# Attention in pairs of heads as blocks of TensorE's order, and small tables loaded later on another queue, in a hybrid decoder layer

## The chip, the cores and the metric

One core of a Trainium2 chip runs the whole layer in one launch. The metric is the device time of that core in microseconds (us). The kernel before took 1037.85 us (median of three runs, 1037.11 to 1038.55).

The engines are named as the profile names them: PE (TensorE matmul) and PEld (its weight loads), DVE (VectorE), ACT (ScalarE), POOL (GpSimd), SP (SyncE, which issues most DMAs). A "weight matmul" below is a matmul of one of the big projections. "fp32r" is the single-pass format of the split operands; a plain fp32 matmul shows as two records (two passes) in the trace.

## What is computed

One layer over 256 tokens and 2048 channels. An RMS norm feeds one input projection (`w_in`) whose columns are the inputs of three branches and their gates: (A) attention with 8 heads of 128, (B) attention with 16 query heads of 64, 4 key/value heads, a window of 128 and sinks, (C) a short convolution with a gated linear recurrence. Each branch is multiplied by a SiLU gate and projected, the sum goes through `w_out`, and a second gated stage and a final norm follow. With 256 tokens both attentions are, for the later 128 queries, scores against all 256 keys, and for the first 128 queries scores against 128 keys. Cut to the attention of branch B:

```python
s = einsum('bnqhgd,bnlhd->bhgnql', qb, kband) * scale + bias
s = where(mask, s, NEG)
p = softmax(concatenate([s, sink_col], -1), -1)[..., :-1]
out = einsum('bhgnql,bnlhd->bnqhgd', p, vband)
```

The bias is a table of 32 buckets per head, looked up by distance.

## The kernel before

All projections are fp32 matmuls done as three fp32r matmuls (`mm3`, L114): each operand is split into a high part (a cast on ACT, L110 for weights) and a low part (a subtraction on DVE, L111), and hi·hi, hi·lo and lo·hi are summed in PSUM. `project_turned` (L157) does the same for results with channels in the rows, with one 512-column matmul (L164) and one 256-column matmul (L166). A weight tile of 1024 columns is loaded by SP into one of four `wraw` buffers, split into one of four `wsp` buffers, and feeds 12 weight matmuls of 512 columns. The code is written stage by stage; a scheduler that simulates the engines then fixes each engine's order, so that small matmuls of the attentions stand between weight matmuls of the merge that runs at the same time (`merge`, L574: branch C's merge around attention A, branch A's merge around attention B). An engine runs its list strictly in order.

`attention` (L431) takes heads two by two (`ha`), but each head of a pair has its own steps on PE: scores (L451, `mm3` of 256 columns, and L452, a plain fp32 matmul of 128 columns for the first 128 queries) into `s_`, softmax (L456 to L476 on DVE and ACT), three transposes of 128x128 (L479) into `pt_`, copies and a split of the result, then the values (L490 to L496) into `py_`. In branch B (`dh` = 64) the scores use 64 rows of the array, the upper half for one head and the lower half for the other; the values fill 64 columns; the second head of a pair skips the split and uses plain fp32 matmuls (L495, L496). All small PSUM tiles (`aux`, L68) share four buffers.

At the start seven dummy matmuls `busy` (L261) run while the first data come. POOL issues the loads of the small tables `tab`, `convw`, `sinkb` (L83, L301) there, and of `onehot` and `maskv` (L318, L319) in the second chunk of the input projection, where a list of hooks (L346) puts small work between weight tiles.

Of the kernel before, what the change touches and what calls it, by code (L numbers as in the profile page):

```python
# [11 lines left out]
F32 = mybir.dt.float32  # L12
# [34 lines left out]
def trunk(ctx: ExitStack, tc: tile.TileContext, x, xt, p, table, onehot, maskv, w_in, sinks, conv, w_ri, vec, fin, w_br,  # L47
# [31 lines left out]
    nc.vector.memset(half_c, -0.5)  # L79

    def load(src, n, name, parts=P):
        t = const.tile([parts, n], F32, name=name)
        nc.gpsimd.dma_start(t, src)  # L83
        return t
# [84 lines left out]
    def unit(name):  # L169
        return block(f"{name}_hi", F32R), block(f"{name}_lo", F32R)  # L170
# [129 lines left out]
    sinkb = const.tile([P, NB], F32, name="sinkb")  # L300
    nc.gpsimd.dma_start(sinkb, bass.AP(tensor=sinks.tensor, offset=sinks.offset, ap=[[0, P], [1, NB]]))  # L301
    acc = temp("acc").rearrange("p k t -> p (k t)")
# [39 lines left out]
    def decay():  # L342
        softplus_neg(sp8)
        nc.vector.tensor_scalar_mul(sp8, sp8, LRU_C)

    second_ps = in_chunk(hooks={2: lambda: squares(0), 4: lambda: squares(1), 6: lambda: squares(2), 8: lambda: squares(3),  # L346
                                10: norm_rows, 12: bias_rows, 14: decay})
# [82 lines left out]

    def attention(nheads, dh, qk_of, row_of, v_of, gate, bias0, sink, name):  # L431
        z = unit(f"z{name}")
        per = P // dh
        st = [small.tile([P, nheads, NH], F32, tag=f"st{i}{name}", name=f"st{i}{name}", bufs=1) for i in range(3)]
        den, mx, sk = st
        q_last = k_last = v_last = None
        for h0 in range(0, nheads, 4):
            bias = bias_tile(bias0 + h0, 4, f"bias_{name}{h0}")
            for ha in (h0, h0 + 2):
                pr = slice(ha, ha + 2)  # L440
                es = []
                for j in range(2):
                    (q, k), rows_of = qk_of(ha + j), row_of(ha + j)
                    if q is not q_last:
                        q_last = q
                        qs = split_small(q[:, P:SEQ], f"q_{name}{ha + j}", "q", P)
                    if k is not k_last:
                        k_last = k
                        ks = split_small(k, f"k_{name}{ha + j}")
                    sc = aux(f"s_{name}{ha + j}")  # L450
                    mm3(sc[:, :SEQ], [t[rows_of] for t in qs], [t[rows_of] for t in ks], True, True)  # L451
                    nc.tensor.matmul(sc[:, SEQ : SEQ + P], q[rows_of, 0:P], k[rows_of, 0:P], start=True, stop=True)  # L452
                    e = small.tile([P, SEQ + P], F32, tag="e", name=f"e_{name}{ha + j}", bufs=4)
                    b = bias[:, ha - h0 + j]
                    for c, (o, w, rev) in enumerate(((0, SEQ, b[:, ::-1]), (SEQ, P, b[:, P - 1 :: -1]))):
                        nc.vector.tensor_tensor_reduce(e[:, o : o + w], sc[:, o : o + w], rev, op0=ALU.add, op1=ALU.max,  # L456
                                                       scale=1.0, scalar=-3.0e38,
                                                       accum_out=mx[:, ha + j, c : c + 1])
                    es.append(e)
                if sink is not None:  # L460
                    nc.vector.tensor_tensor(mx[:, pr], mx[:, pr], sink[:, pr].unsqueeze(2).to_broadcast([P, 2, NH]), op=ALU.max)
                    nc.vector.tensor_tensor(sk[:, pr], sink[:, pr].unsqueeze(2).to_broadcast([P, 2, NH]), mx[:, pr], op=ALU.subtract)
                    nc.scalar.activation(sk[:, pr], sk[:, pr], AF.Exp)
                nc.vector.tensor_scalar_mul(mx[:, pr], mx[:, pr], -1.0)
                for j in range(2):
                    for c, o, w in ((0, 0, SEQ), (1, SEQ, P)):
                        nc.scalar.activation(es[j][:, o : o + w], es[j][:, o : o + w], AF.Exp,
                                             bias=mx[:, ha + j, c : c + 1], accum_out=den[:, ha + j, c : c + 1])
                if sink is not None:
                    nc.vector.tensor_add(den[:, pr], den[:, pr], sk[:, pr])  # L470
                nc.vector.reciprocal(den[:, pr], den[:, pr])
                py = aux(f"py_{name}{ha}")
                for j in range(2):
                    e = es[j]
                    for c, o, w in ((0, 0, SEQ), (1, SEQ, P)):
                        nc.vector.tensor_scalar_mul(e[:, o : o + w], e[:, o : o + w], den[:, ha + j, c : c + 1])  # L476
                    pt = aux(f"pt_{name}{ha + j}")
                    for c, o in enumerate((SEQ, 0, P)):
                        nc.tensor.transpose(pt[:, c * P : (c + 1) * P], e[:, o : o + P], ident)  # L479
                    v0, v1 = v_of(0, ha + j), v_of(1, ha + j)  # L480
                    part = slice(j % per * dh, (j % per + 1) * dh)
                    o = j // per * SEQ
                    if part.start == 0:
                        w1 = small.tile([P, P], F32, tag="w1", name=f"w1_{name}{ha + j}")
                        nc.scalar.copy(w1, pt[:, SEQ : SEQ + P])
                        w0 = split_small(pt[:, :SEQ], f"w0_{name}{ha + j}", "w")
                        if v0 is not v_last:
                            v_last = v0
                            vs = split_small(v0, f"v_{name}{ha + j}", "v", dh)
                        mm3(py[part, o : o + SEQ], vs, w0, True, False)  # L490
                    else:
                        w = small.tile([P, SEQ + P], F32, tag="w", name=f"w_{name}{ha + j}")
                        nc.scalar.copy(w, pt[:, : SEQ + P])
                        w1 = w[:, SEQ:]
                        nc.tensor.matmul(py[part, o : o + SEQ], v0, w[:, :SEQ], start=True, stop=False)  # L495
                    nc.tensor.matmul(py[part, o + P : o + SEQ], v1, w1, start=False, stop=True)  # L496
                n = 2 // per
                kt = ha // per
                nc.vector.tensor_tensor(gate[:, cols(kt, n)], py[:, : n * SEQ], gate[:, cols(kt, n)], op=ALU.mult)
                split_act(z, kt, n, gate[:, cols(kt, n)])  # L500
        return z
# [13 lines left out]
    def branch_a(between):  # L515
        qT, kT, g = block("qa"), block("ka"), block("ga")
        turned(ktiles(qT), 4, DA ** -0.5)
        between()
        turned(ktiles(kT), 4)
        between()  # L520
        silu(ktiles(g), 2, "ga0")
        between()
        silu(ktiles(g)[:, 4:, :], 2, "ga1")
        va = [[vh[:, c, h * DA : (h + 1) * DA] for h in range(NA)] for c in range(NH)]
        qa, ka = ([ktiles(t)[:, h, :] for h in range(NA)] for t in (qT, kT))
        return attention(NA, DA, lambda h: (qa[h], ka[h]), lambda h: slice(0, P),
                         lambda c, h: va[c][h], g, 0, None, "a")

    def branch_b():
# [7 lines left out]

        def kv_of(h):
            return B_ORDER[h] // (NB // NKV)

        def part(h):
            return slice(h % 2 * DB, (h % 2 + 1) * DB)

        qb = [ktiles(qT)[:, i, :] for i in range(NB // 2)]
        kb = [kT[:, i, :] for i in range(2)]
        vb = [[vt[:, c, i * DB : (i + 1) * DB] for i in range(NKV)] for c in range(NH)]

        return attention(NB, DB, lambda h: (qb[h // 2], kb[kv_of(h) // 2]), part,
                         lambda c, h: vb[c][kv_of(h)], g, NA, sinkb, "b")

# [208 lines left out]
```

## Time and profile before

| | |
|---|---|
| median of three runs | 1037.85 us |
| the profiled execution's own time | 1037.24 us |
| its span, first to last instruction | 1035.5 us |
| PE busy | 1022.5 us (99%) |
| DVE, ACT, POOL busy | 637.9, 537.6, 43.6 us |
| attention B on PE | 540 to 702 us, among weight matmuls |
| attention A on PE | 255 to 366 us |

The profiled execution is 0.61 us below the median. Matmuls are pipelined: a record's own length overlaps the next one, so a matmul's price is read as the distance from its start to the next start.

### The profile page before, as it was taken

How to read it: one execution, taken by the hardware profiler on the slowest of the kernel's cores; microseconds unless marked ns; L12 is line 12 of the kernel's file. 1: busy time of each engine (PE TensorE's matmuls, PEld its weight loads, DVE VectorE, ACT ScalarE, POOL GpSimd, SP SyncE). 2: the span in 40 equal slices, each digit the busy share in tenths (PEclk: the TensorE clock that was granted, in tenths of full speed). 3: DMA queues.
4: the chain of work that ended last, by engine and by line, in shares of the span. 5: the costliest groups of instructions: out<-in, count | busy, mean ns of one | idle time of the engine just before them, and what ended most of it. 6: DMA issues, size and time to landing. Idle time of an engine off the chain costs nothing.

```text
span 1035.5 us, 13720 instructions
## 1 busy us (share of the span) xinstructions
PE 1022.5 (99%) x5222; PEld 861.2 (83%) x5222; DVE 637.9 (62%) x891; ACT 537.6 (52%) x763; POOL 43.6 (4%) x36
## 2 busy tenths in 40 slices
PE   9999999999999999999999999999999999999996
PEld 6888888888888888889887777778888888888886
DVE  6768666769777554455566656655554555554564
ACT  6644455585577543444446564653444444555552
POOL 0000000001000000000000100000000000000122
PEclk9999999999999999999999999999999999999999
DMA  8776555545754656555655554455565855556652
GB/s 286 229 264 190 193 179 173 179 144 168 232 187 152 195 184 192 194 187 189 193 185 163 179 168 146 158 169 181 186 197 183 278 189 191 187 183 226 198 186 82
DMA packets 57288, 195.34 MB, mean 189 GB/s; under 512 B 6321, under 2 KB 10217, under 8 KB 56965
## 3 DMA queue, kind: packets, MB, share of 16 engines
q1 hardware_dynamic: 52704, 186.67, 55.7%
q10 hardware_dynamic: 4356, 7.67, 2.3%
q8 instruction: 41, 0.67, 0.3%
q0 software_dynamic: 160, 0.11, 0.1%
q14 instruction: 27, 0.21, 0.1%
HBM read 192.30 MB, written 2.13 MB: 188 GB/s over the span
## 4 chain that ended last, share of the span: by engine, by line
PE 97%; DMA 1%; issue 1%; DVE 0%; SPq 0%; ACT 0%; POOLq 0%; POOL 0%; DVEq 0%
PE ps_in L164 21%; PE ps_in L166 11%; PE ps_in L116 10%; PE ps_in L117 10%; PE ps_in L118 10%; PE ps_out L116 3%; PE ps_out L118 3%; PE ps_out L117 3%; PE ps_pg L117 3%; PE ps_pg L116 3%; PE ps_pg L118 3%; PE ps_bra L116 2%; PE ps_bra L118 1%; PE ps_bra L117 1%; PE ps_brc L116 1%; PE ps_brc L118 1%
## 5 line engine op out<-in xcount | busy, mean ns | idle before, releaser
L111 DVE TENSOR_TENSOR wl_in<-r_in,wh_in 128x1024 fp32r<-128x1024 f32 (+1 forms) x235 | 292.8, 1251 | 189.6 <-ACT wh_in L110 189.1
L110 ACT CAST wh_in<-r_in 128x1024 fp32r<-128x1024 f32 (+1 forms) x235 | 243.5, 1039 | 274.8 <-PE ps_in L164 133.6
L164 PE MATMUL ps_in<-h,wh_in 128*128 128x512 f32 x928 | 290.1, 393 | 0.0
L166 PEld LDWEIGHTS ps_in<-h,wl_in 128*128 128x128 f32 x928 | 173.8, 188 | 41.5 <-DVE wl_in L111 2.0
L116 PE MATMUL ps_in<-wh_in,h 128*128 128x512 f32 (+1 forms) x480 | 186.8, 389 | 1.2 <-ACT wh_in L110 1.2
L166 PE MATMUL ps_in<-h,wl_in 128*128 128x256 f32 x928 | 185.4, 280 | 1.1 <-DVE wl_in L111 1.1
L117 PE MATMUL ps_in<-wl_in,h 128*128 128x512 f32 (+1 forms) x480 | 186.1, 388 | 0.2 <-DVE wl_in L111 0.2
L118 PE MATMUL ps_in<-wh_in,h 128*128 128x512 f32 (+1 forms) x480 | 184.5, 384 | 0.0
L164 PEld LDWEIGHTS ps_in<-h,wh_in 128*128 128x128 f32 x928 | 142.4, 188 | 0.3
L116 PEld LDWEIGHTS ps_in<-wh_in,h 128*128 128x128 f32 x480 | 90.7, 189 | 20.6 <-ACT wh_in L110 2.3
L117 PEld LDWEIGHTS ps_in<-wl_in,h 128*128 128x128 f32 x480 | 90.8, 189 | 19.3 <-DVE wl_in L111 1.6
L118 PEld LDWEIGHTS ps_in<-wh_in,h 128*128 128x128 f32 x480 | 90.8, 189 | 17.5
L111 DVE TENSOR_TENSOR wl_pg<-r_pg,wh_pg 128x1024 fp32r<-128x1024 f32 x32 | 39.8, 1243 | 39.2 <-ACT wh_pg L110 39.2
L111 DVE TENSOR_TENSOR wl_out<-r_out,wh_out 128x1024 fp32r<-128x1024 f32 x32 | 39.2, 1224 | 37.1 <-ACT wh_out L110 37.1
L110 ACT CAST wh_out<-r_out 128x1024 fp32r<-128x1024 f32 x32 | 33.7, 1054 | 42.5 <-PE ps_out L118 36.5
L117 PE MATMUL ps_pg<-wl_pg,x_hi 128*128 128x512 f32 (+1 forms) x160 | 55.3, 347 | 0.0
L118 PE MATMUL ps_pg<-wh_pg,x_lo 128*128 128x512 f32 (+1 forms) x160 | 55.3, 347 | 0.0
L116 PE MATMUL ps_pg<-wh_pg,x_hi 128*128 128x512 f32 (+1 forms) x160 | 55.3, 347 | 0.0
L110 ACT CAST wh_pg<-r_pg 128x1024 fp32r<-128x1024 f32 x32 | 33.7, 1053 | 39.6 <-PE ps_pg L118 36.8
L117 PE MATMUL ps_out<-wl_out,m_hi 128*128 128x512 f32 x128 | 50.1, 391 | 0.0
L116 PE MATMUL ps_out<-wh_out,m_hi 128*128 128x512 f32 x128 | 49.9, 390 | 0.0
L118 PE MATMUL ps_out<-wh_out,m_lo 128*128 128x512 f32 x128 | 49.8, 389 | 0.0
(274 smaller groups left out, 1279.7 us busy)
## 6 DMA issues: line engine op xcount, KB each, us to landing
r_in<-w_in_dram SPq DMA_DIRECT2D x229, 512.0 KB, 3.5
r_out<-w_out_dram SPq DMA_DIRECT2D x32, 512.0 KB, 3.4
r_pg<-w_pg_dram SPq DMA_DIRECT2D x24, 512.0 KB, 4.2
r_brc<-w_br_dram SPq DMA_DIRECT2D x16, 512.0 KB, 3.5
r_bra<-w_br_dram SPq DMA_DIRECT2D x16, 512.0 KB, 4.3
r_brb<-w_br_dram SPq DMA_DIRECT2D x16, 512.0 KB, 4.2
r_pg<-w_pgt_dram SPq DMA_DIRECT2D x8, 512.0 KB, 4.3
bias_b<-rv_d ACTq DMA_DIRECT2D x4, 512.0 KB, 4.8
```

Source lines behind the costliest of these rows:

```text
L110: casts.append(nc.scalar.copy(hi[:, c], r[:, c]).ins)
L111: nc.vector.tensor_tensor(lo[:, c], r[:, c], hi[:, c].bitcast(F32), op=ALU.subtract)
L116: nc.tensor.matmul(ps, ah, bh, start=first, stop=False)
L117: nc.tensor.matmul(ps, ah, bl, start=False, stop=False)
L118: nc.tensor.matmul(ps, al, bh, start=False, stop=last)
L164: nc.tensor.matmul(ps[:, j, :], wh[:, cs[j]], h_both[k], start=k == 0, stop=False)
L166: nc.tensor.matmul(ps[:, j, SEQ:], wl[:, cs[j]], h_act[k][0], start=False, stop=k == KD - 1)
```

## The change

`attention` is replaced by `attention_heads` (branch A) and `attention_pairs` (branch B). Both tie the scores of a pair, its six transposes and its values each into one chain on PE (`chained`), so that the scheduler places three blocks per pair and nothing else stands inside a block. In A the matmuls are the same in number and form. In B the scores of the first 128 queries become three fp32r matmuls of 128 columns per head instead of one plain fp32 matmul, and the two heads alternate matmul by matmul; the values of both heads become three matmuls of 512 columns over 128 value columns (both key/value heads at once) and three of 2x128 columns, all in fp32r; the result is taken from the matching 64 rows by two multiplications. Two of the six transposes of a pair go to unused columns of the score tiles, so that one `pt_` tile serves both heads. The splits on ACT and DVE become wider to match (512 columns, two low parts of 128, queries of 256 columns).

The table loads of POOL move to ACT's queue: `tab`, `convw`, `sinkb` at hook 0 of the second chunk, `onehot` and `maskv` where they were. One dummy matmul is added (seven to eight). The scratch for software DMAs is cut to 8192 bytes.

```diff
     def load(src, n, name, parts=P):
         t = const.tile([parts, n], F32, name=name)
-        nc.gpsimd.dma_start(t, src)
+        late_loads.append((t, src))
...
-    for i in range(7):
+    for i in range(8):
         nc.tensor.matmul(busy[:, :P], ones, ones, start=True, stop=True)
...
-        nc.gpsimd.dma_start(oneh, onehot)
-        nc.gpsimd.dma_start(rv, maskv)
+        nc.scalar.dma_start(oneh, onehot)
+        nc.scalar.dma_start(rv, maskv)
...
+    def tables():
+        for dst, src in late_loads:
+            nc.scalar.dma_start(dst, src)
...
+    def chained(calls):
+        ins = None
+        for call in calls:
+            with tc.issue_after(ins) if ins is not None else nullcontext():
+                ins = call().ins
...
+    def transposes(pt, scs, es):
+        dst = {(j, o): d for j in range(2) for o, d in ((SEQ, pt[:, 2 * j * P : (2 * j + 1) * P]),
+                                                        (0, pt[:, (2 * j + 1) * P : (2 * j + 2) * P]),
+                                                        (P, scs[j][:, SEQ + P :]))}
+        chained([(lambda d=dst[j, o], j=j, o=o: nc.tensor.transpose(d, es[j][:, o : o + P], ident))
+                 for j in (1, 0) for o in (SEQ, P, 0)])
...
+    def attention_pairs(qb, kb, vt, gate):
...
+        for i in range(NB // 2):
...
+            qs = split_small(qb[i], f"q_b{i}", "q")
+            scs = [aux(f"s_b{i}{j}") for j in range(2)]
+            chained([mm(scs[j][:, o : o + w], qs[a][rows_of[j], q0 : q0 + P], ks[b][rows_of[j], :w], n == 0, n == 2)
+                     for o, w, q0 in ((0, SEQ, P), (SEQ, P, 0)) for n, (a, b) in enumerate(((1, 0), (0, 1), (0, 0)))
+                     for j in range(2)])
...
+            softmax_rows(es, scs, bias[:, i % 2 * 2 : i % 2 * 2 + 2], mx[:, pr], den[:, pr], sk[:, pr], sinkb[:, pr])
+            pt, py = aux(f"pt_b{i}"), aux(f"py_b{i}")
+            transposes(pt, scs, es)
+            w0 = split_small(pt, f"w0_b{i}", "w", CW)
+            w1 = [small.tile([P, 2, P], F32R, tag=f"u{c}", name=f"w1{c}_b{i}") for c in "hl"]
+            for j in range(2):
+                nc.scalar.copy(w1[0][:, j, :], scs[j][:, SEQ + P :])
+                nc.vector.tensor_tensor(w1[1][:, j, :], scs[j][:, SEQ + P :], w1[0][:, j, :].bitcast(F32), op=ALU.subtract)
+            late = py.rearrange("p (j t) -> p j t", j=2)[:, :, P:]
+            passes = ((0, 1), (0, 0), (1, 0))
+            chained([mm(py, vs[0][a], w0[b], n == 0, False) for n, (a, b) in enumerate(passes)]
+                    + [mm(late, vs[1][a], w1[b], False, n == 2) for n, (a, b) in enumerate(passes)])
+            for j in range(2):
+                gj = gate[rows_of[j], cols(i)]
+                nc.vector.tensor_tensor(gj, py[rows_of[j], j * SEQ : (j + 1) * SEQ], gj, op=ALU.mult)
+            split_act(z, i, 1, gate[:, cols(i)])
```

PE's order in attention B, before: the second transposes and part of the values of the first pair, then the scores of the second pair (`s_b_4859` and `s_b_4867` are its two heads), with `ps_in` weight matmuls ahead and behind.

```order
L116 MATMUL py_b_4821<-w_b_hi,v_b_hi 64x256
L479 MATMUL pt_b_4844<-ident,e_b_4808 128x128
L117 MATMUL py_b_4821<-w_b_lo,v_b_hi 64x256
L118 MATMUL py_b_4821<-w_b_hi,v_b_lo 64x256
L496 MATMUL py_b_4821<-w_b_4828,kvb 64x128
L479 MATMUL pt_b_4844<-ident,e_b_4808 128x128 x2
L116 MATMUL s_b_4859<-k_b_hi,q_b_hi 128x256
L117 MATMUL s_b_4859<-k_b_lo,q_b_hi 128x256
L118 MATMUL s_b_4859<-k_b_hi,q_b_lo 128x256
L452 MATMUL s_b_4859<-kvb,qb 128x128
L116 MATMUL s_b_4867<-k_b_hi,q_b_hi 128x256
L117 MATMUL s_b_4867<-k_b_lo,q_b_hi 128x256
```

The same place now: three 512-column value matmuls and three of 2x128 columns of the first pair, then the scores of the second pair, heads alternating (`s_b_4845` and `s_b_4846`).

```order
L469 MATMUL py_b_4814<-w_b_lo,v_b_hi 128x512
L469 MATMUL py_b_4814<-w_b_hi,v_b_hi 128x512
L469 MATMUL py_b_4814<-w_b_hi,v_b_lo 128x512
L469 MATMUL py_b_4814<-w1l_b_4826,v_b_hi 128x2x128
L469 MATMUL py_b_4814<-w1h_b_4825,v_b_hi 128x2x128
L469 MATMUL py_b_4814<-w1h_b_4825,v_b_lo 128x2x128
L469 MATMUL s_b_4845<-k_b_hi,q_b_lo 128x256
L469 MATMUL s_b_4846<-k_b_hi,q_b_lo 128x256
L469 MATMUL s_b_4845<-k_b_lo,q_b_hi 128x256
L469 MATMUL s_b_4846<-k_b_lo,q_b_hi 128x256
L469 MATMUL s_b_4845<-k_b_hi,q_b_hi 128x256
L469 MATMUL s_b_4846<-k_b_hi,q_b_hi 128x256
```

The six transposes of a pair now stand alone, 26 to 31 weight matmuls ahead of the values block of the same pair and 45 to 59 behind its scores.

ACT's order at the start of the second chunk, before: casts of weight tiles and the first sum of squares.

```order
L110 CAST wh_in_7_278<-r_in_7_276 128x1024
L110 CAST wh_in_0_310<-r_in_0_308 128x1024
L110 CAST wh_in_1_328<-r_in_1_326 128x1024
L199 ACTIVATE acc<-x_87 128x1024
L110 CAST wh_in_2_347<-r_in_2_345 128x1024
```

The same place now: three table loads stand between the casts of the first and the second tile.

```order
L112 CAST wh_in_7_279<-r_in_7_277 128x1024
L112 CAST wh_in_0_308<-r_in_0_306 128x1024
L350 DMA tab<-table_dram 32x24
L350 DMA convw<-conv_dram 128x32
L350 DMA sinkb<-sinks_dram 128x16
L112 CAST wh_in_1_329<-r_in_1_327 128x1024
L201 ACTIVATE acc<-x_87 128x1024
```

The loads left POOL's list at the start, and `onehot` and `maskv` stand on ACT behind the cast of the seventh tile.

## Rows read from the trace of the kernel before

**Rows 1.** The page: busy time of the engines, and the chain that ended last.

```profile
PE 1022.5 (99%) x5222; PEld 861.2 (83%) x5222; DVE 637.9 (62%) x891; ACT 537.6 (52%) x763; POOL 43.6 (4%) x36
...
PE 97%; DMA 1%; issue 1%; DVE 0%; SPq 0%; ACT 0%; POOLq 0%; POOL 0%; DVEq 0%
```

**Rows 2.** Timeline of attention B, one pair: start, length, engine, line, tiles, shapes.

```profile
559.08 0.39 PE L116 MATMUL ps_in<-wh_in,h 128*128 128x512 f32 x1
...
560.58 0.38 PE L116 MATMUL s_b<-k_b_hi,q_b_hi 64*128 64x256 f32 x1
560.80 0.27 PE L117 MATMUL s_b<-k_b_lo,q_b_hi 64*128 64x256 f32 x1
560.81 0.38 PE L116 MATMUL s_b<-k_b_hi,q_b_hi 64*128 64x256 f32 x1
...
561.27 0.38 PE L452 MATMUL s_b<-kvb,qb 64*128 64x128 f32 x2
561.58 0.50 PE L117 MATMUL ps_in<-wl_in,h 128*128 128x512 f32 x1
561.91 0.40 PE L118 MATMUL ps_in<-wh_in,h 128*128 128x512 f32 x1
```

**Rows 3.** Timeline of PE around the second head's values of that pair.

```profile
564.91 0.39 PE L116 MATMUL ps_in<-wh_in,h 128*128 128x512 f32 x1
...
566.36 0.40 PE L118 MATMUL ps_in<-wh_in,h 128*128 128x512 f32 x1
```

**Rows 4.** Timeline of PE: eight transposes in a row, in the merge.

```profile
742.60 0.39 PE L118 MATMUL ps_in<-wh_in,h 128*128 128x512 f32 x1
742.83 1.03 PE L566 MATMUL tp_m<-ident,merged 128*128 128x128 f32 x8
...
743.93 0.40 PE L117 MATMUL ps_in<-wl_in,h 128*128 128x512 f32 x1
```

**Rows 5.** Timeline of PE: the narrowest matmuls of the kernel, one column each.

```profile
44.77 0.50 PE L216 MATMUL tot_in<-ones,acc 128*128 128x1 f32 x4
...
45.46 0.40 PE L117 MATMUL ps_in<-wl_in,h 128*128 128x512 f32 x1
```

**Rows 6.** Timeline of the next pair's first transposes and the last split behind them.

```profile
571.87 0.49 PE L479 MATMUL pt_b<-ident,e_b 128*128 128x128 f32 x3
...
572.15 1.23 DVE L111 TENSOR_TENSOR wl_in<-r_in,wh_in 128x1024 fp32r<-128x1024 f32 x1 [1.87 <-ACT wh_in L110]
...
573.30 0.42 DVE L185 TENSOR_TENSOR w_b_lo<-pt_b,w_b_hi 128x256 fp32r<-128x256 f32 x1
```

**Rows 7.** Timeline of the first 14 us; in brackets the idle time and its releaser.

```profile
5.03 0.79 PE L116 MATMUL ps_in<-wh_in,h 128*128 128x512 f32 x1 [0.61 <-ACT wh_in L110]
...
7.20 0.63 PE L117 MATMUL ps_in<-wl_in,h 128*128 128x512 f32 x1
...
7.63 0.63 PE L118 MATMUL ps_in<-wh_in,h 128*128 128x512 f32 x1
...
10.17 0.51 ACT L190 ACTIVATE h<-x,vecs 128x256 fp32r<-128x256 f32 x1 [2.28 <-DMA x<-xt_dram]
10.44 0.40 PE L118 MATMUL ps_in<-wh_in,h 128*128 128x512 f32 x1
...
12.48 0.39 PE L118 MATMUL ps_in<-wh_in,h 128*128 128x512 f32 x1
```

**Rows 8.** Windows at the start: stretch, granted clock, DMA busy share, GB/s.

```profile
2.00:5.00 3.00, 1.00 1.01 280
5.00:10.00 5.00, 1.00 0.82 187
10.00:14.00 4.00, 1.00 1.04 407
```

**Rows 9.** DMA issues by line: KB each, us from issue to landing.

```profile
sinkb<-sinks_dram POOLq DMA_DIRECT2D x1, 8.0 KB, 7.4
```

**Rows 10.** Timeline of ACT early in the second chunk.

```profile
26.95 1.05 ACT L110 CAST wh_in<-r_in 128x1024 fp32r<-128x1024 f32 x1 [1.11 <-DMA r_in<-w_in_dram]
```

More of the change, by code (lines that the diff above doesn't have):

```diff
@@ L429, in branch_c, with softmax_rows @@
         yield z
[L431 to L438, printed above, removed]
+    def softmax_rows(es, scs, bias, mx, den, sk, sink):
+        for j in range(2):
+            b = bias[:, j]
+            for c, (o, w, rev) in enumerate(((0, SEQ, b[:, ::-1]), (SEQ, P, b[:, P - 1 :: -1]))):
+                nc.vector.tensor_tensor_reduce(es[j][:, o : o + w], scs[j][:, o : o + w], rev, op0=ALU.add, op1=ALU.max,
+                                               scale=1.0, scalar=-3.0e38, accum_out=mx[:, j, c : c + 1])
+        if sink is not None:
+            nc.vector.tensor_tensor(mx, mx, sink.unsqueeze(2).to_broadcast([P, 2, NH]), op=ALU.max)
+            nc.vector.tensor_tensor(sk, sink.unsqueeze(2).to_broadcast([P, 2, NH]), mx, op=ALU.subtract)
+            nc.scalar.activation(sk, sk, AF.Exp)
+        nc.vector.tensor_scalar_mul(mx, mx, -1.0)
+        for j in range(2):
+            for c, o, w in ((0, 0, SEQ), (1, SEQ, P)):
+                nc.scalar.activation(es[j][:, o : o + w], es[j][:, o : o + w], AF.Exp,
+                                     bias=mx[:, j, c : c + 1], accum_out=den[:, j, c : c + 1])
+        if sink is not None:
+            nc.vector.tensor_add(den, den, sk)
+        nc.vector.reciprocal(den, den)
+        for j in range(2):
+            for c, o, w in ((0, 0, SEQ), (1, SEQ, P)):
+                nc.vector.tensor_scalar_mul(es[j][:, o : o + w], es[j][:, o : o + w], den[:, j, c : c + 1])
@@ new lines, in probs, with mm @@
+    def probs(name):
+        return small.tile([P, SEQ + P], F32, tag="e", name=name, bufs=4)
+    def chained(calls):
[3 more added lines that the diff above has]
+                ins = call().ins
+    def mm(out, a, b, start, stop):
+        return lambda: nc.tensor.matmul(out, a, b, start=start, stop=stop)
+    def transposes(pt, scs, es):
[4 more added lines that the diff above has]
+                 for j in (1, 0) for o in (SEQ, P, 0)])
@@ L439, in attention, with attention_heads @@
+    def attention_heads(qa, ka, va, gate):
+        z = unit("za")
+        mx, den = (small.tile([P, NA, NH], F32, tag=f"st{i}a", name=f"st{i}a", bufs=1) for i in range(2))
+        for h0 in range(0, NA, 4):
+            bias = bias_tile(h0, 4, f"bias_a{h0}")
             for ha in (h0, h0 + 2):
                 pr = slice(ha, ha + 2)
-                es = []
-                for j in range(2):
[L443 to L500, printed above, removed]
+                scs = [aux(f"s_a{ha + j}") for j in range(2)]
+                es = [probs(f"e_a{ha + j}") for j in range(2)]
+                qs = [split_small(qa[ha + j][:, P:SEQ], f"q_a{ha + j}", "q", P) for j in range(2)]
+                ks = [split_small(ka[ha + j], f"k_a{ha + j}") for j in range(2)]
@@ new lines, in attention_heads @@
+                chained([mm(scs[j][:, :SEQ], qs[j][a], ks[j][b], n == 0, n == 2)
+                         for j in (1, 0) for n, (a, b) in enumerate(((1, 0), (0, 1), (0, 0)))]
+                        + [mm(scs[j][:, SEQ : SEQ + P], qa[ha + j][:, 0:P], ka[ha + j][:, 0:P], True, True) for j in range(2)])
+                softmax_rows(es, scs, bias[:, ha - h0 : ha - h0 + 2], mx[:, pr], den[:, pr], None, None)
+                pt, py = aux(f"pt_a{ha}"), aux(f"py_a{ha}")
+                transposes(pt, scs, es)
@@ new lines, in attention_heads @@
+                vs = [split_small(va[0][ha + j], f"v_a{ha + j}", "v", DA) for j in range(2)]
+                w1 = small.tile([P, 2, P], F32, tag="uh", name=f"w1_a{ha}")
+                for j in range(2):
+                    nc.scalar.copy(w1[:, j, :], scs[j][:, SEQ + P :])
+                w0 = [t.rearrange("p (j t) -> p j t", j=2) for t in split_small(pt, f"w0_a{ha}", "w", CW)]
+                o = [slice(j * SEQ, (j + 1) * SEQ) for j in range(2)]
+                chained([mm(py[:, o[j]], vs[j][a], w0[b][:, j, :], n == 0 and j == 0, False)
+                         for j in range(2) for n, (a, b) in enumerate(((0, 1), (0, 0), (1, 0)))]
+                        + [mm(py[:, j * SEQ + P : (j + 1) * SEQ], va[1][ha + j], w1[:, j, :], False, j == 1) for j in range(2)])
@@ L536, in branch_b @@
         silu(ktiles(g), 4, "gb")
[L538 to L542, printed above, removed]
         qb = [ktiles(qT)[:, i, :] for i in range(NB // 2)]
         kb = [kT[:, i, :] for i in range(2)]
-        vb = [[vt[:, c, i * DB : (i + 1) * DB] for i in range(NKV)] for c in range(NH)]
-        return attention(NB, DB, lambda h: (qb[h // 2], kb[kv_of(h) // 2]), part,
-                         lambda c, h: vb[c][kv_of(h)], g, NA, sinkb, "b")
+        return attention_pairs(qb, kb, vt, g)
     merged = []
```

27 lines of the change are left out of this document (22 added, 5 removed).

## The prediction, made before the changed kernel ran

> **What bounds the kernel now.** I read the busy times first, then the chain that ended last, then the timelines where the change works. PE is busy for 1022.5 of 1035.5 us, and the chain lies on PE for 97% of the span [rows 1]; DVE, at 637.9 us, is next. So time is won only where PE's own matmuls cost less, or where PE stands idle. PE idles little: most of it is in the first 12.5 us [rows 7]. What the attentions cost PE is read from a stretch as the time between the starts of the weight matmuls around it, less 0.227 us for each of those (0.23 from one to the next in [rows 4]).
>
> **Attention B, before.** One pair has three stretches on PE. From 559.08 to 561.91 [rows 2] there are 2.83 us with two weight matmuls, so 2.38 us for three transposes, the first head's values and the next pair's scores. From 564.91 to 566.36 [rows 3] there are 1.45 with two, so 1.00 us for the second head's values in plain fp32. Three more transposes stand alone: eight take 743.93 - 742.60 = 1.33 with two weight matmuls, so 0.88, or 0.11 each [rows 4]; three are 0.33 us. The pair costs 3.71 us, eight pairs 29.7 us.
>
> **Attention B, after.** The order has three blocks per pair. Six transposes are 6 x 0.11 = 0.66 us. The values are three 512-column matmuls at 0.227 and three of 256 columns at 0.12 (four places from 560.80 to 561.27 are 0.117 each [rows 2]), 1.04 us; the 64-column form, with its change of the array's layout, is gone. For the scores, before, there are 1.33 us from 560.58 to 561.91 [rows 2], of which 0.227 are a weight matmul, so 1.10. I add 0.10 for entering the 64-row form, because leaving it costs that (0.33 instead of 0.23 from 561.58 to 561.91): 1.20 us. In this block the two heads already run together where they overlap: matmuls of the two row halves start at 560.80 and 560.81 [rows 2]. Because the first head stands ahead of the second, the block has seven places, the first included. With the heads alternating, six places hold twelve matmuls, if a 128-column fp32r place costs no more than the 0.117 of the others. That takes away one place: 1.20 - 0.12 = 1.08 us.
>
> A pair is then 2.78 us, and eight save 8 x 0.93 = 7.4 us, all on PE, the engine that sets the end. Two of these prices the trace of before does not show. A 128-column fp32r matmul lies between 0.115, the distance of one-column matmuls (four take 45.46 - 44.77 - 0.227 = 0.46 us [rows 5], so something other than columns is the floor), and twice 0.117 if it runs like a two-pass fp32 one; I take 0.117, since the floor is in sight and the 256-column one needs no more. At the other end the saving is 3 x 0.117 x 8 = 2.8 us less. Whether two heads overlap throughout a chained block is the other: without overlap six places become twelve, 6 x 0.117 x 8 = 5.6 us less. [Rows 2] show the overlap in a block that was not even written for it, so I take it in full.
>
> The Trainium skill (TensorE: Matmul & The Clock Gate, Back-to-back issue gap) gives about 81 ns for a stream of 128-column matmuls with their weight loads. By that, three places would be 3 x (0.117 - 0.081) x 8 = 0.9 us cheaper in sum. The one-column matmuls at 0.115 us speak against it here, and the sum stays without it.
>
> **Attention A.** Matmuls and forms are the same, only their order is closed up. I take 0, with 0 to 0.3 us of gain for fewer changes of form.
>
> **DVE and ACT in the attentions.** The wider splits add work off PE: per pair of B about a microsecond on DVE (the last split, 0.42 us for 256 columns [rows 6], covers 512; two subtractions of 128 columns and half a query split come on top). DVE has 40% of its time free [rows 1], and nothing is charged for this; the cover is the weight matmuls between blocks. From the transposes at 571.87 to the end of the last split at 573.30 + 0.42 = 573.72 [rows 6] there are 1.85 us; twice that for twice the width is 3.7 us. The order leaves 26 to 31 weight matmuls in that place, 5.9 us and more. What stands queued on DVE behind the new subtractions, which wait for the transposes, are the low parts of coming weight tiles; on ACT their casts. PE would wait for those if they came late.
>
> **The start.** The first weight matmul waits 0.61 us for ACT's cast at 5.03 [rows 7]; the eighth dummy (two passes) fills a part of this gap and costs nothing. Up to 10 us the matmuls stand 0.43 us apart (7.20 to 7.63 [rows 7]), which is the 1.2 GHz level (the column of the granted clock prints 1.00 there too [rows 8], but the spacing is double); later ones 0.227. From 10.44 to 12.48 three weight matmuls take 2.04 us [rows 7] instead of 0.68: 1.36 us of waiting, and the cause is in the same rows, ACT's h at 10.17 after 2.28 us of waiting for x. The DMA engines moved 280 GB/s before 5 us, 187 from 5 to 10, and 407 from then on [rows 8]. In the slow stretch POOL's small tables are under way (`sinkb` needs 7.4 us to land [rows 9]). If they are the cause, without them the 1.1 MB that the dip cost (5 us x 220 GB/s) arrive 2.7 us earlier at 407 GB/s, more than PE can use: the 1.36 us go, and PE's own half-speed matmuls are next. I take 1.4 us, with 0 to 3.0 as bounds (below). In the second chunk three table loads stand ahead of a cast on ACT's queue; no row here prices the issue of a DMA on ACT, so I bound it by the 0.51 us of a whole activation [rows 7], 1.5 us for three, of which ACT's idle time before the cast at 26.95 covers 1.11 [rows 10]. I charge nothing for the rest, since the tiles after it are split ahead of their use; without any cover it would be 1.5 us once. `onehot` has PE's bias matmul behind it, ten microseconds later in the order; nothing is charged.
>
> The Trainium skill (DMA: Bandwidth & Descriptors, Queues, rings and completion order) says that all queues run on the same 16 engines, which take turns between them packet by packet, so that another queue moves contention rather than removes it. By that the dip would come again near 27 us, where a cast already waits for its DMA [rows 10]. The gain of 1.4 us would then be given back; this is rival 2.
>
> **Sum.** 1037.24 - 7.4 - 0 - 1.4 = 1028.4 us against the profiled execution; that one is 0.61 us below its median, so I expect a median of 1029.0.
>
> **Rivals.** Rival 1: the 128-column passes cost double: 1029.0 + 2.8 = 1031.8. For it speaks that no row shows this form; against it that a floor near 0.115 explains both known widths.
>
> Rival 2: the start gains nothing, because the dip has another cause (SP's own queue is held up in it) or is only moved: 1029.0 + 1.4 = 1030.4. For it: cause and dip coincide in time, no more.
>
> Rival 3: PE's clock rises sooner. The eighth dummy shortens PE's idle time ahead of the first weight matmul from 0.61 to some 0.2 us, and no wait follows. If the clock rose eight matmuls sooner, each of these would cost 0.2 us less: 1029.0 - 1.6 = 1027.4. Against it: before, the level rose only at about 10 us, after 9 us of nearly unbroken work.
>
> Rival 4: the two row halves don't overlap: 1029.0 + 5.6 = 1034.6. [Rows 2] speak against it.
>
> Rival 5: slower, the values blocks wait. A chained block can't start in part; it needs the last split of both heads. If on DVE one weight split of 1.23 us [rows 6] in each of the twelve blocks comes between, and the room of 5.9 us is already used, PE loses 12 x 1.23 = 14.8 us: 1043.8, slower than before. It outweighs the gain from (1037.85 - 1029.0) / 12 = 0.74 us per block on. Against it: 3.7 us are needed of 5.9.
>
> **How the numbers follow.** A difference below 0.2% (2.1 us) can't be told from none. Chances: the forecast (1028 to 1030) 0.46; rival 2 0.19; rival 3 0.10; rival 1 0.10; rival 4 0.04; blocks that wait a little (1031 to 1035) 0.04; rival 5 and other waits of more than that 0.07, of which 0.04 end slower and 0.03 within 0.2%. The range leaves out the far side of rivals 4 and 5 and some of rival 3: 1026.2 to 1033.8. Faster by more than that: all the others, 0.93; the same 0.03; slower 0.04.
>
> **What would show it.** Right: blocks of six `pt_b`/`s_b` transposes 0.66 us long; scores with pairs of starts less than 0.02 us apart and six places; values of about 1.04 us; no wait of PE inside branch B; at the start DMA near 400 GB/s from 4 us on and no PE wait at 11 us. Wrong: PE idle ahead of `py_b` or of a weight matmul behind it with DVE as releaser (rival 5); 0.23 us between 128-column scores (rival 1); twelve starts about 0.117 apart (rival 4); the wait for x still at 10 us (rival 2).

## The result

The changed kernel takes **1027.05 us** (median of four runs, 1026.47 to 1027.34) beside 1037.76 us for the kernel before (four runs, 1037.11 to 1038.55). The ratio is 0.9896, with a 95% interval from 0.9879 to 0.9913: 10.7 us less. Forecast were 1029.0 us with a range from 1026.2 to 1033.8, so the time is inside, 1.95 us below the forecast. It is outside the narrow band of 1028 to 1030 that had a chance of 0.46, and stands next to the 1027.4 of rival 3.

### The profile page after: what moved, and what is told of

It is laid out like the page before. It is cut to its first block, busy times and chain, and to the rows that moved or that the text cites. A ratio compares the mean times of both kernels' runs of the same rounds, so it can differ in the third digit from the quotient of the medians.

```text
span 1025.0 us, 13714 instructions
## 1 busy us (share of the span) xinstructions
PE 1012.6 (99%) x5216; PEld 860.1 (84%) x5216; DVE 647.1 (63%) x913; ACT 542.4 (53%) x763; POOL 43.2 (4%) x31
## 4 chain that ended last, share of the span: by engine, by line
PE 97%; DMA 1%; issue 1%; DVE 0%; SPq 0%; ACT 0%; POOLq 0%; POOL 0%; DVEq 0%
PE ps_in L166 21%; PE ps_in L168 11%; PE ps_in L119 10%; PE ps_in L118 10%; PE ps_in L120 10%; PE ps_out L118 3%; PE ps_out L120 3%; PE ps_out L119 3%; PE ps_pg L119 3%; PE ps_pg L118 3%; PE ps_pg L120 3%; PE ps_bra L120 1%; PE ps_bra L119 1%; PE ps_brc L119 1%; PE ps_bra L118 1%; PE ps_brc L120 1%
```

## The profile after

The page of the changed kernel, answering [rows 1]: PE has lost 9.9 us of busy time and six records, DVE has gained 9.2 us, and the chain lies on PE as before. The span is 1025.0 us, 10.5 less.

```profile
PE 1012.6 (99%) x5216; PEld 860.1 (84%) x5216; DVE 647.1 (63%) x913; ACT 542.4 (53%) x763; POOL 43.2 (4%) x31
...
PE 97%; DMA 1%; issue 1%; DVE 0%; SPq 0%; ACT 0%; POOLq 0%; POOL 0%; DVEq 0%
```

Where the 10.5 us lie is read from first starts of the same tiles in both traces (for the kernel before, `tot_in` is in [rows 5] and the first `tp_m` in [rows 4]). The first scores of B, before:

```profile
540.56 0.38 PE L116 MATMUL s_b<-k_b_hi,q_b_hi 64*128 64x256 f32 x1
```

and after:

```profile
43.33 0.50 PE L218 MATMUL tot_in<-ones,acc 128*128 128x1 f32 x4
...
538.95 0.39 PE L469 MATMUL s_b<-k_b_hi,q_b_lo 64*128 64x256 f32 x2
...
732.64 1.03 PE L597 MATMUL tp_m<-ident,merged 128*128 128x128 f32 x8
```

| from, to | before | after | difference |
|---|---|---|---|
| start to first column sum (`tot_in`) | 44.77 | 43.33 | -1.44 |
| `tot_in` to first scores of A | 210.56 | 210.56 | 0 |
| attention A, to first scores of B | 285.23 | 285.06 | -0.17 |
| **attention B**, to first `tp_m` | 202.27 | 193.69 | **-8.58** |
| `tp_m` to the end of the span | 292.64 | 292.33 | -0.31 |

The last line is not PE's: from the first `tp_m` to the start of PE's last matmul there are 283.01 us in both traces. The 0.3 us lie behind it, and they go with the tables, not with the attention: this stretch takes 292.3 us in the traces with the tables in the second chunk (e1 and e2 below too, which have the old attention) and 292.6 to 292.8 in those that issue them at the start (before, e3, e4, e7, e8). In return the time outside the span is longer: time less span has a median of 1.8 to 1.9 us over the runs of each of those five kernels, and of 2.3 for the changed kernel, e1 and e2. The two profiled executions thus differ by 9.9 us (1037.24 and 1027.34) where their spans differ by 10.5. No row shows what fills the time outside the span.

Attention B, one pair: the timeline of PE of the changed kernel (start, length, engine, line, tiles, shapes), values and then the next pair's scores. It answers [rows 2, 3].

```profile
558.98 0.39 PE L118 MATMUL ps_in<-wh_in,h 128*128 128x512 f32 x1
...
560.13 0.28 PE L469 MATMUL py_b<-w1h_b,v_b_lo 128*128 128x256 f32 x1
560.34 0.39 PE L469 MATMUL s_b<-k_b_hi,q_b_lo 64*128 64x256 f32 x2
560.56 0.28 PE L469 MATMUL s_b<-k_b_lo,q_b_hi 64*128 64x256 f32 x2
560.67 0.28 PE L469 MATMUL s_b<-k_b_hi,q_b_hi 64*128 64x256 f32 x2
560.79 0.22 PE L469 MATMUL s_b<-k_b_hi,q_b_lo 64*128 64x128 f32 x2
560.85 0.27 PE L469 MATMUL s_b<-k_b_lo,q_b_hi 64*128 64x128 f32 x2
560.96 0.27 PE L469 MATMUL s_b<-k_b_hi,q_b_hi 64*128 64x128 f32 x2
561.16 0.50 PE L119 MATMUL ps_in<-wl_in,h 128*128 128x512 f32 x1
561.50 0.40 PE L120 MATMUL ps_in<-wh_in,h 128*128 128x512 f32 x1
```

Each `x2` is the two heads of a pair, 0.001 to 0.005 us apart. From 558.98 to 561.50 there are 2.52 us with two weight matmuls, 2.07 without. The six transposes of a pair, as a block:

```profile
574.44 0.39 PE L120 MATMUL ps_bra<-wh_bra,za_lo 128*128 128x512 f32 x1
574.67 0.27 PE L475 MATMUL pt_b<-ident,e_b 128*128 128x128 f32 x1
...
...
575.56 0.40 PE L119 MATMUL ps_bra<-wl_bra,za_hi 128*128 128x512 f32 x1
```

1.12 us with two weight matmuls, 0.67 without. A pair costs 0.666 + 2.065 = 2.73 us (before 3.72). The last split of this pair, in DVE's timeline, answers [rows 6]:

```profile
577.92 0.68 DVE L187 TENSOR_TENSOR w_b_lo<-pt_b,w_b_hi 128x512 fp32r<-128x512 f32 x1
```

and the values that need it, in PE's:

```profile
582.41 0.39 PE L469 MATMUL py_b<-w_b_lo,v_b_hi 128*128 128x512 f32 x1
```

The split ends at 578.60, 3.8 us ahead of its use. Over the eight pairs this room is 3.0 to 4.4 us, and PE waits nowhere in attention B.

The start answers [rows 7]. PE's timeline (in brackets the idle time ahead and its releaser):

```profile
6.07 0.40 PE L120 MATMUL ps_in<-wh_in,h 128*128 128x512 f32 x1
6.30 0.40 PE L118 MATMUL ps_in<-wh_in,h 128*128 128x512 f32 x1
...
15.30 0.39 PE L118 MATMUL ps_in<-wh_in,h 128*128 128x512 f32 x1
16.22 0.50 PE L119 MATMUL ps_in<-wl_in,h 128*128 128x512 f32 x1 [0.53 <-DVE wl_in L113]
```

ACT's timeline there:

```profile
10.67 0.51 ACT L192 ACTIVATE h<-x,vecs 128x256 fp32r<-128x256 f32 x1 [0.68 <-DMA x<-xt_dram]
```

The matmuls stand 0.23 us apart (the 2.4 GHz level) from 6 us on, not from 10. Then they wait for data in small pieces, four times between 8.5 and 16.2 us, the last one 0.69 us beyond the usual distance. The window (stretch, length, granted clock, DMA busy share, GB/s) answers [rows 8]:

```profile
5.00:10.00 5.00, 1.00 0.91 303
```

303 GB/s stand between 5 and 10 us where 187 stood. In the second chunk, on ACT and its queue (answers [rows 10]):

```profile
23.13 0.38 ACTq L350 DMA_DIRECT2D tab<-table_dram  x1
...
23.53 0.45 ACTq L350 DMA_DIRECT2D convw<-conv_dram  x1
...
25.73 1.05 ACT L112 CAST wh_in<-r_in 128x1024 fp32r<-128x1024 f32 x1 [1.31 <-DMA r_in<-w_in_dram]
```

An issue takes 0.38 to 0.45 us, and the cast behind them waits for its weight tile anyway. PE waits nowhere between 18 and 40 us.

## Experiments on the start

All times are medians of runs taken beside the kernel before on the same chip; a ratio's interval is 95%.

**e1, e2, e3: the start alone.** All three are the kernel before. e1 has the table loads as changed and eight dummies, e2 only the table loads, e3 only the eighth dummy.

```diff
-        nc.gpsimd.dma_start(t, src)           # e1, e2
+        late_loads.append((t, src))
...
-    for i in range(7):                        # e1, e3
+    for i in range(8):
```

> The kernel before with the table loads moved to ACT's queue in the second chunk and eight dummies; the attentions as before. Theory (start and attention add up): 1.4 us faster than before, about 1036.3, the first tot_in matmul 1.4 us earlier than before's 44.77. Rival (part of the start's gain needs the new attention): less than 0.7 us.

> As e1 with seven dummies. Theory (the DMA dip is the cause): 1.4 us faster than before all the same, no dip from 5 to 10 us (about 300 GB/s), even if the weight matmuls stand 0.43 us apart until about 10 us. Rival (the clock's earlier rise is the cause): no gain, 1037.8, with the dip gone.

> The kernel before with eight dummies instead of seven, tables on POOL's queue at the start. Theory: no gain, 1037.8, since the data come no sooner; the spacing of the first weight matmuls may fall to 0.23 us early, and the time goes into longer waits for x. Rival (clock): the spacing falls early and 1.4 us are won.

Measured beside 1037.50 us for the kernel before: e1 1035.61 us, ratio 0.9979 [0.9970, 0.9988]; e2 1035.66, 0.9979 [0.9971, 0.9988]; e3 1037.47, 1.0003 [0.9994, 1.0012]. The window of e2 and, below it, of e3:

```profile
5.00:10.00 5.00, 1.00 0.88 288
```

```profile
5.00:10.00 5.00, 1.00 0.84 209
```

The table loads are the whole gain of the start, the dummy is none of it; the gain is 1.8 us where 1.4 were expected. In e3 the clock rose at 7.3 us (the spacing falls to 0.23 us), three microseconds sooner than before, and PE then stood idle for 2.12 us waiting for a cast, whose data came no sooner. PE in e3 behind that wait:

```profile
11.28 0.50 PE L116 MATMUL ps_in<-wh_in,h 128*128 128x512 f32 x1 [2.12 <-ACT wh_in L110]
...
13.50 0.39 PE L117 MATMUL ps_in<-wl_in,h 128*128 128x512 f32 x1
```

**e8 and e7: the queue or the moment.** e8 is the changed kernel with the three tables issued by ACT at the start; e7 has them in the code of the second chunk as changed, but issued by POOL.

```diff
-        late_loads.append((t, src))           # e8
+        nc.scalar.dma_start(t, src)
...
-            nc.scalar.dma_start(dst, src)     # e7
+            nc.gpsimd.dma_start(dst, src)
```

> The changed kernel with the three tables on ACT's hardware queue at the start, behind vecs. Theory (the software queue was the disturbance): the DMA rate from 5 to 10 us stays near 300 GB/s and the time within 0.5 us of the changed kernel. Rival (small packets at the start disturb on any queue): the dip to about 190 GB/s is back, and the time is 1.4 us longer, 1028.5.

> The changed kernel with its five table loads in the second chunk as before, but issued by POOL, on the software queue. The tables alone brought 1.8 us when they left the start, and on ACT's queue at the start they cost nothing beside the changed kernel (1027.18 against 1027.05 us), so the software queue was the disturbance. Theory: the software queue slows the weight loads wherever it runs, but in the second chunk PE has buffers ahead of it: 1026.7 to 1027.5 us, and DMA shows a dip near 27 us. Rival: a dip there reaches PE too, as at the start: 1028.3 us and more, with a wait of PE for a weight tile between 25 and 40 us.

Measured: e8 1027.18 us (1026.85 to 1027.27), ratio 0.9898 [0.9881, 0.9914], the changed kernel's time. e7 1030.06 (1029.56 to 1030.46), 0.9926 [0.9913, 0.9938]: 3.0 us slower than the changed kernel. But e7 did not test what it was written for. Its edit moves three loads, not the five that the expectation names (`onehot` and `maskv` stayed on ACT's queue), and POOL waits for nothing ahead of them, so they were issued at once, from 1.31 us on, and not in the second chunk. The timeline of POOL in e7:

```profile
2.56 0.53 POOL L350 DMA_DIRECT2D sinkb<-sinks_dram  x1
```

the windows of e7:

```profile
5.00:10.00 5.00, 1.00 0.81 205
10.00:14.00 4.00, 0.67 1.02 401
```

and PE in e7 around the wait:

```profile
11.48 0.80 PE L118 MATMUL ps_in<-wh_in,h 128*128 128x512 f32 x1 [2.65 <-ACT wh_in L112]
...
12.80 0.63 PE L120 MATMUL ps_in<-wh_in,h 128*128 128x512 f32 x1
13.23 0.63 PE L118 MATMUL ps_in<-wh_in,h 128*128 128x512 f32 x1
...
14.86 0.40 PE L119 MATMUL ps_in<-wl_in,h 128*128 128x512 f32 x1
```

So e7 and e8 are the same tables at the same time, on the software queue and on ACT's hardware queue: 2.9 us between them. The software queue was the disturbance, not the tables' bytes and not the moment; in e8 the window from 5 to 10 us shows 268 GB/s, 205 in e7. Part of e7's loss is the clock: after the wait of 2.65 us the matmuls stand 0.43 us apart, the 1.2 GHz level, until 14.5 us. Seven distances behind the wait take 3.38 us (11.48 to 14.86), against 2.22 in e3 (11.28 to 13.50), where the level stayed up. What the software queue does elsewhere was not tried.

**e4: attention alone.** The changed kernel with the start of before (tables, `onehot` and `maskv` on POOL, seven dummies).

```diff
-        late_loads.append((t, src))
+        nc.gpsimd.dma_start(t, src)
...
-    for i in range(8):
+    for i in range(7):
...
```

> The changed kernel with before's start (tables on POOL's queue at the start, seven dummies). Theory: the attention alone gives 8.6 us in branch B and 0.2 in A by the trace of after, so about 1028.8; the tot_in matmul stands where it stood before. Rival (the queues matter in the attention too): over 1.5 us away from that.

Measured: 1030.31 us (1028.9 to 1031.73), 0.9930 [0.9916, 0.9943]. Attention B takes 193.69 us in its trace, to the hundredth what it takes in the changed kernel. The time is 1.5 us above the expectation, which just meets the rival's number, but the cause is not in the attention: the first `tot_in` comes only at 46.44, 1.7 us later than in the kernel before, whose start has the same instructions. In e4 the clock was up by 6 us, PE then waited 1.17 and 1.38 us for casts, and after the second wait it worked at the lower level from 11.9 to 15.3 us:

```profile
10.00:14.00 4.00, 0.74 1.03 404
```

So the start with the software queue has no fixed price. The first `tot_in` stands at 44.77 and 44.65 us in the traces of before and e3, and at 46.44 and 45.93 in those of e4 and e7, where the clock fell. The changed kernel's cut of the scratch for software DMAs (8192 bytes) separates the two pairs: e4 and e7 have it, before and e3 do not. No run varies it alone, so whether it is part of the higher price is open.

**e11: the changed kernel once more**, beside e12 (below). Its trace bears on what the clock is worth here.

> The changed kernel itself, on the same chip and beside e12_plain_again: 1026.5 to 1027.4 us as before.

Measured: 1026.46 us (1026.22 to 1027.19), 0.9891 [0.9875, 0.9908]. Its PE rows at the start:

```profile
9.33 0.63 PE L118 MATMUL ps_in<-wh_in,h 128*128 128x512 f32 x1
9.76 0.63 PE L119 MATMUL ps_in<-wl_in,h 128*128 128x512 f32 x1
...
10.87 0.39 PE L119 MATMUL ps_in<-wl_in,h 128*128 128x512 f32 x1
11.09 0.39 PE L120 MATMUL ps_in<-wh_in,h 128*128 128x512 f32 x1
```

This time the level rose only after 10 us, and PE then worked up to 16.8 us without a wait. The first `tot_in` starts at 43.30, against 43.33 in the trace in which the level rose at 6 us. In these two the arrival of data sets the start, and the clock only decides whether PE is slow or waits. Where the level falls behind a wait, with data at hand, it does cost: some 1.2 us in e7.

## Experiments on attention B

**e5: heads in turn.** The changed kernel with the scores of one head behind those of the other, as before.

```diff
-                     for o, w, q0 in ((0, SEQ, P), (SEQ, P, 0)) for n, (a, b) in enumerate(((1, 0), (0, 1), (0, 0)))
-                     for j in range(2)])
+                     for j in range(2)
+                     for o, w, q0 in ((0, SEQ, P), (SEQ, P, 0)) for n, (a, b) in enumerate(((1, 0), (0, 1), (0, 0)))])
```

> The changed kernel with B's scores head after head instead of alternating; the same twelve matmuls. Theory (the row halves overlap by themselves and only one place is lost): a scores block 0.06 to 0.12 us longer, 0.5 to 1.0 us in all, 1027.6 to 1028.1. Rival (only alternating matmuls overlap): six more places, 0.5 us a block, 4 us in all, 1031.

Measured: 1029.3 us (1029.1 to 1029.44), 0.9919 [0.9904, 0.9933]. The timeline of a scores block:

```profile
560.00 0.38 PE L469 MATMUL s_b<-k_b_hi,q_b_lo 64*128 64x256 f32 x1
...
560.34 0.28 PE L469 MATMUL s_b<-k_b_hi,q_b_hi 64*128 64x256 f32 x1
560.34 0.38 PE L469 MATMUL s_b<-k_b_hi,q_b_lo 64*128 64x256 f32 x2
...
560.98 0.27 PE L469 MATMUL s_b<-k_b_hi,q_b_hi 64*128 64x128 f32 x1
561.18 0.50 PE L119 MATMUL ps_in<-wl_in,h 128*128 128x512 f32 x1
```

The second head begins with the first head's third matmul, and at the end it stands alone. A block takes 0.36 us more (1.39 against 1.03), 2.9 us in eight; attention B takes 196.47 us, 2.8 more, and the time is 2.25 more. Each of twelve matmuls in a place of its own would have cost about twice that, so the halves overlap in this order too, but only in part: the time lies between the theory and the rival.

**e9: values as before.** The changed kernel with the values head by head over 64 columns, the second head and the first queries in plain fp32, but in one chain next to the scores.

```diff
-            chained([mm(py, vs[0][a], w0[b], n == 0, False) for n, (a, b) in enumerate(passes)]
-                    + [mm(late, vs[1][a], w1[b], False, n == 2) for n, (a, b) in enumerate(passes)])
+            last = chained([mm(py[r0, :SEQ], vs[0][0][:, r0], w0[0], True, False),
...
+                     mm(py[r1, :SEQ], vt[:, 0, c[1]], w[:, :SEQ], True, False),
+                     mm(py[r1, P:SEQ], vt[:, 1, c[1]], w[:, SEQ:], False, True)])
```

> The changed kernel with B's values as before: head by head into 64 columns, the second head in plain fp32. Theory (the joint values block is most of the gain): values cost 0.8 us more per pair, 6.5 us in all, so about 1033.5. Rival (the scores' alternation and the closed blocks are most of it): under 2.5 us slower than the changed kernel.

Measured: 1029.37 us (1028.83 to 1029.74), 0.9919 [0.9904, 0.9934], only 2.3 us more than the changed kernel, as the rival had it. Its timeline, in one of the six pairs whose values, all but the first, stay together:

```profile
579.30 0.87 PE L469 MATMUL py_b<-w_b,kvb 128*64 128x128 f32 x6
580.10 0.39 PE L469 MATMUL s_b<-k_b_hi,q_b_lo 64*128 64x256 f32 x2
```

and the same passes in the kernel before, first and second head:

```profile
559.85 0.43 PE L496 MATMUL py_b<-w_b,kvb 128*64 128x128 f32 x2
560.22 0.44 PE L479 MATMUL pt_b<-ident,e_b 128*128 128x128 f32 x2
...
565.23 0.65 PE L495 MATMUL py_b<-w_b,kvb 128*64 128x256 f32 x2
...
566.02 0.50 PE L117 MATMUL ps_in<-wl_in,h 128*128 128x512 f32 x1
```

Six plain passes of both heads take 0.80 us; apart, they took 0.37 (559.85 to 560.22) and 0.79 (565.23 to 566.02) in the kernel before, 1.16. The first of them start 0.007 us apart: the two halves of columns run beside each other as the row halves do. Such a pair costs some 0.14 us more than the wide form. In the first and the last pair weight matmuls came between the values, and these two cost 0.7 and 1.1 us more. Six times 0.14, 0.7 and 1.1 make 2.6; attention B is 2.5 us longer (196.20).

**e6: without the ties.** `chained` issues its calls without tying them.

```diff
-            with tc.issue_after(ins) if ins is not None else nullcontext():
-                ins = call().ins
+            call()
```

> The changed kernel without the ties that hold a block together; the scheduler is free, and its order differs only by a weight matmul or two inside the transposes. Theory (the forms of the matmuls are the gain, not the closed order): the same time within 0.5 us, 1027. Rival (closed blocks are the gain): over 2 us slower.

Measured: 1026.9 us (1026.36 to 1027.64), 0.9896 [0.9881, 0.9911]; attention B 193.77 us. Written in this order, the matmuls stay together without ties, but for one transpose of each pair, which stands a weight matmul ahead of the other five. So the ties are not needed; what an open order would cost, e6 does not test.

**e10 and e12: plain scores.** The changed kernel, with the scores of the first 128 queries as one plain fp32 matmul per head again, heads next to each other; e12 is e10 once more, on the chip of e11.

```diff
+                    + [mm(scs[j][:, SEQ : SEQ + P], qb[i][rows_of[j], 0:P], kb[g][rows_of[j], 0:P], True, True)
+                       for j in range(2)])
```

> The changed kernel, but in branch B the scores of the first 128 queries are one plain fp32 matmul per head again, as before; the heads still stand next to each other. Theory: with the two row halves beside each other the two passes of both heads take two places of about 0.11 us, against 0.058 and 0.109 for the first two of the three places now, and the last place goes: the block stays within 0.07 us of 1.033, the time within 0.6 us of 1027.05, 1026.4 to 1027.7. Then the gain of the scores lies in the order of the heads and not in the format. Rival: two-pass matmuls of the two heads don't run beside each other: four places of 0.11 instead of two, 0.22 us more in each of eight blocks, 1028.8 us.

> The kernel of e10_plain_scores again, beside the changed kernel. In e10's trace a scores block takes 0.972 us against 1.033, 0.061 less, 0.5 us in eight blocks; the other half of its lead of 1.0 us lay in the start (first tot_in at 42.66 against 43.30), where both kernels have the same instructions. Theory: the blocks are real and the start is chance from run to run, so 0.3 to 0.7 us ahead of e11_after_again. Rival: the start is part of it, 0.8 us or more. Second rival: nothing is left of it, below 0.2 us.

Measured: e10 1026.08 us (1025.85 to 1026.29), 0.9887 [0.9872, 0.9902]; e12 1026.07 (1025.81 to 1026.85), 0.9890 [0.9875, 0.9904], 0.39 less than e11 beside it, within the 0.3 to 0.7 of its theory. e10's timeline:

```profile
560.71 0.38 PE L469 MATMUL s_b<-kvb,qb 64*128 64x128 f32 x4
561.02 0.50 PE L118 MATMUL ps_in<-wh_in,h 128*128 128x512 f32 x1
```

The first pass of both heads and the second take two places, 0.31 us to the weight matmul with the exit from the form, where the three fp32r places take 0.37 (560.79 to 561.16). A block takes 0.972 us instead of 1.033, eight times 0.061 are 0.49 us, and attention B takes 193.21 us, 0.48 less. The trace thus shows a gain of half a microsecond, though the ranges of the times of e11 and e12 overlap. It is the fastest version of this study, with the same attention otherwise. e10's time is 0.3 us below the range of its theory, and its first `tot_in` stands at 42.89 us against 43.33 (the 42.66 in e12's expectation is that of e5's trace): the start varies by that much between traces with the same instructions.

## Why the prediction was right, and where it was not

**Attention B** was the term that mattered: 7.4 us forecast, 8.6 measured. The forms priced from [rows 2, 4] held: six transposes 0.67 (0.66), values 1.05 where they stand alone (1.04). Two sizes were off. The scores block takes 1.03 instead of 1.08 us, because the second of the three 128-column places starts only 0.06 us behind the first: 0.4 us in eight blocks. The distance of 0.115 us that the prediction took for a floor is thus none where the halves alternate. And the pair of before was taken from one pair; over all pairs its stretches add to 29.9 us, not 29.7. These stretches give 29.90 - 21.86 = 8.04. The rest was missed: behind each stretch the weight matmuls stand a little further apart for some places. Over the 756 weight matmuls that both traces have here, the second to eighth distances behind a stretch hold 0.86 us above 0.227 before and 0.43 after. The prediction charged only the first. That 25 stretches have become 17 would explain it, but this is argued: e6 has 25 again, eight of them a single transpose, and the same 0.43.

**Why it is cheaper** was half wrong. The prediction put the gain of the values down to the wide form, with the 64-column form gone. By its own rows the values of before cost 1.85 us a pair (2.38 - 1.20 - 0.33 for the first head, 1.00 for the second). In e9 the same matmuls, put together, cost 1.16 to 1.20, only some 0.14 us per pair more than the wide form. What was dear was their being spread: two heads' column halves that could not run beside each other (0.36 us of it), and, as far as the rows tell, the way into and out of the form in two places instead of one. e6 shows that no ties are needed for it. In the scores e5 and e10 show that the order of the heads is worth 2.8 us and the fp32r form costs half a microsecond; the 2.8 are against e5, which has all twelve fp32r matmuls in turn. Against the block that the kernel before had (1.20 us) the scores gained 0.17 us a pair, 1.4 in all.

The Trainium skill (TensorEngine Tiling (Array Packing), Key Properties) says that changing the tiling mode drains the engine. The rows agree at the scores: 0.21 us from the last value matmul to the first score where 0.12 is usual, and 0.20 on the way out. The 0.34 instead of 0.23 between the first two weight matmuls behind it, from which the prediction took its 0.10 for a change of form, is no sign of one: in the kernel before 0.33 us, from 45.13 to 45.46, also stand behind the one-column matmuls of [rows 5], which use the full array. That the entry costs 0.09 us all the same is luck.

**From the parts to 1.95 us.** Attention B, the start, A and the tail were 1.7 us better than forecast in the span. The longer time outside the span takes 0.6 back. The forecast had added 0.61 us because the profiled execution of before lies below its median; that of the changed kernel lies 0.29 above its own, which gives 0.9. This last part is chance between executions.

**The start** was forecast at 1.4 us, and the traces give 1.44, but that is partly luck. The mechanism is right (e2, e8), and the 1.36 us of waiting in [rows 7] are gone; in their place come a sooner clock and four smaller waits for data, or (e11) a late clock and none. The sign "DMA near 400 GB/s from 4 us on" did not come: 303 stand there, about half of the dip, and some waits stayed. The forecast "PE's own half-speed matmuls are next" is seen in e11, and in e2 up to 8.9 us. And the price is not a constant: 1.8 us in the kernel before (1037.5 - 1035.66, e2), 3.0 and 3.3 in the changed kernel (e7, e4), where the clock fell behind a wait.

**Attention A** gained 0.17 us of the 0 to 0.3 allowed. The last 0.3 us behind `tp_m` were not forecast; they belong to the tables' place, as said above.

**The rivals.** Rival 1 (128-column places cost double) fell: 0.06 and 0.11 us. Rival 2 (start gains nothing, or the dip only moves) fell with e2. The Trainium skill (DMA: Bandwidth & Descriptors, Queues, rings and completion order) has all queues share 16 engines packet by packet; by that alone the same bytes at the same time should cost about the same in e7 and e8. They differ by 2.9 us, and the measurement decides: sharing the engines does not explain it. The tables' own packets do not either: in the first 14 us the packets of POOL's queue take 3.9% of the engines' time in e7, those of ACT's queue 2.9% in e8. How the software queue slows the others stays open. Rival 3 (clock sooner) happened, and its 1027.4 is nearer to the time than the forecast, but the clock was worth nothing (e3, e11). Rival 4 (no overlap) fell: pairs start within 0.005 us. Rival 5 (values wait) fell: 3.0 to 4.4 us of room were left, though one pair needed 4.5 us for its splits, not 3.7.

## What to carry to other kernels

Matmuls that use half of the array's rows or columns should stand next to those of the opposite half, in one place, and for row halves alternately: that, more than their number format, set the cost of this attention. Count the stretches of small matmuls, with the slower weight matmuls behind each. In this kernel small loads at the start belonged on a hardware queue. And ask what a slower clock costs where PE, not the data, sets the pace: here it cost nothing ahead of a wait for data, and about a microsecond behind one.

## What was not expected of the hardware

- With small loads of 27 KB in all on the software queue the DMA engines moved 177 to 209 GB/s from 5 to 10 us (before, e3, e4, e7), against 268 to 303 without (e8, e2, the changed kernel). This cost 1.8 to 3.3 us.
- The granted clock fell back to its lower level after waits of PE of 2.65 us (e7) and of 1.17 and 1.38 us (e4), for about 3 us each time (0.67 and 0.74 in the window from 10 to 14 us); in e3 it stayed up after a wait of 2.12 us. In the changed kernel it rose at about 6 us in one trace and after 10 in another. In the first microseconds the column of the granted clock prints 1.00 at either spacing.
- Of three 128-column fp32r places in a row with alternating halves, the second follows 0.06 us behind the first, the third 0.11 behind the second.
- In e5 the second head's first matmul starts beside the first head's third (560.34 us), ahead of three matmuls that stand before it in the order (560.45 to 560.62). PE does not start its list strictly in order here.
